# A transformer layer on one core: the two products with the same weights joined into one wide product, the first loads put in a new order

## The chip, the core and the metric

The kernel runs on one core of one Trainium2 chip. The core has TensorE (matrix products, written to PSUM), VectorE, ScalarE and GpSimd (element-wise work), and SyncE, whose queue here does nothing but issue loads and stores. The metric is the device time of one execution in microseconds (us), the median of three runs. A separate profiled execution gives the rows that are quoted below; times in them count from the start of its span.

## The reference

One layer, 256 rows of width 2048, all in float32. Three sublayers, each followed by a layer norm of (1.19 x input + result):

```python
h = x @ w_in                               # 2048 -> 7216 columns
(q_a, k_a, v_a, q_b, k_c, v_c, k_s, v_s, k_w, v_w, g_nsa, g_merge) = split(h)
y_a = swa_sink_attention(q_a, k_a, v_a)    # 16 heads, window 128, sinks, relative bias
y_b = nsa_attention(q_b, ...)              # 16 heads: compressed, selected and window keys, gated
merged = sigmoid(g_a) * (y_a @ w_branch_swa) + sigmoid(g_b) * (y_b @ w_branch_nsa)
x1 = layer_norm(ALPHA * x + merged @ w_mix_out)
x2 = layer_norm(ALPHA * x1 + cross_attention(x1, mem))   # 4 heads of 128
out = layer_norm(ALPHA * x2 + square(relu(x2 @ mlp_w1)) @ mlp_w2)   # 2048 -> 8192 -> 2048
```

The compressed keys and values are a small network of their own: 15 overlapping blocks of 32 tokens, 2048 -> 256 -> 64 with gelu between.

## The kernel before

**Split products.** Every large product is made from two parts of each operand: `h` is the value rounded to the format of the fast product, `l` the rest. A product of x and w is then h x xh + h x xl + l x xh. Weights come from memory in chunks of 128 x 1024 values (128 x 1072 for the keys and values). For each chunk ScalarE makes `h` (L168) and VectorE `l` (L169). Activations are split the same way when they are transposed (`hilo`, L322 and L323); `xth` and `xtl` hold the two parts of the transposed x, 16 blocks (k) of 128 x 256.

**Two forms.** `block_x` (`mm_x`, L201 to L208) keeps the activations as the fixed operand and streams up to 512 columns of weights. `block_w` (`mm_w`, L216 to L219) keeps a 128 x 128 tile of weights fixed and streams the 256 rows of x, so its result comes out transposed; it makes three products of 256 columns for each tile and each k, all into the same half of a PSUM bank. It is used for the two query blocks (`evac_qa`, `evac_qb`), the memory's keys and queries (512 columns each) and the first MLP stage (8 blocks of 1024 columns). The key/value chunks (`make_c`, 16 of them, one k each) do both: six products of 432 columns and fifteen of 256.

**Order.** The order of each engine's queue is written by hand. `run_chunks` goes through the list of chunks: it issues loads (five raw buffers), makes the splits up to three chunks ahead, emits the products of this chunk, then, at the end of a block, its evacuation. Chunks marked in `evac_first` leave one split for after the evacuation. Everything else (transposes, softmax, the compression chain) is a generator in `Side`: a `yield "pe"` gives the step that follows its place behind the products of a chunk, a `yield "ev"` before the next chunk's splits, `"ev0"` ahead of the other `"ev"` steps. A yield is thus a slot of the chunk loop, about 2.9 us long.

**The front.** x's first 256 columns, then chunk 0, x's next 256 columns, chunk 1 and so on are issued from SyncE, five loads a chunk; the other 1536 columns of x and a dozen small tables are issued from GpSimd. TensorE transposes x in pairs of blocks between the chunks (`x_side`). `small_start` makes the bias table after four slots.

**The compression chain** (`compress`) runs after the last of eight chunks that are set between those of the first query block: results `hid` copied, transposed on TensorE (`hidt`), gelu on VectorE and ScalarE (L554 to L564), then twelve small products into `kvc` (L570, L573). In the same slots the queries of the first attention are evacuated (`evac_q`, L310 and L315) and stacked (`stack_q`: ScalarE copies at L596, subtractions at L597, every other one on GpSimd).

**Banks.** PSUM has eight banks: four under the tag `acc`, and `lg`, `pt`, `o`, `mi`, which the side work uses. Before the MLP and within it, blocks alternate between the two sets; the blocks before use `acc` only, so that a block can begin a bank only when the block before has been copied out of it.

## Time and profile before

| | |
|---|---|
| median of three runs | 1442.91 us (1441.77 to 1443.74) |
| the profiled execution | 1444.05 us, of it 1442.3 us span |
| TensorE busy | 1412.6 us, 98% |
| VectorE, ScalarE, GpSimd busy | 875.2, 712.0, 174.5 us |
| moved by DMA | 268.58 MB, 186 GB/s over the span |
| mean granted TensorE clock | 0.99 of full |

The records of TensorE's products overlap, since a product starts while the one before drains; what a product costs in a row of them is the distance between two starts, not the length of a record. The granted clock is given as a share of 2.4 GHz.

### The profile page before, as it was taken

What the parts mean: (1) busy time and instruction counts of PE and PEld (TensorE: products, weight loads), DVE (VectorE), ACT (ScalarE), POOL (GpSimd) and SP (SyncE); (2) the same over time, 40 slices, a digit from 0 to 9 for tenths busy, and PEclk for the clock granted to TensorE, in tenths of its full rate; (3) what the DMA queues carried; (4) which work ended last, traced back from release to release, by engine and by line L of the source; (5) the groups of instructions that cost most, each with busy time, mean ns of one, the idle gap of its engine ahead of it and who ended that gap; (6) DMA issues with size and microseconds to landing.
All of it is one profiled execution on the core that took longest, in us unless ns stands there. A gap on an engine that the chain in (4) does not pass through costs nothing.

```text
span 1442.3 us, 22448 instructions
## 1 busy us (share of the span) xinstructions
PE 1412.6 (98%) x8732; PEld 1275.6 (88%) x8732; DVE 875.2 (61%) x1323; ACT 712.0 (49%) x1098; POOL 174.5 (12%) x165
## 2 busy tenths in 40 slices
PE   7999999999999999999999999999999999999996
PEld 6999988888888888899899999999998888888885
DVE  3577887888546466675854444444446555665556
ACT  3465776677444444454444444344445544544452
POOL 3002221221001010130201111011101000000002
PEclk9999999999999999999999999999999999999998
DMA  8765555454766575574355555665657666566552
GB/s 232 228 209 186 161 150 172 146 149 132 248 192 186 190 292 184 164 239 144 132 180 186 180 184 178 190 182 184 183 183 250 193 197 191 176 212 195 192 193 84
DMA packets 96282, 268.58 MB, mean 186 GB/s; under 512 B 9344, under 2 KB 32592, under 8 KB 95408
## 3 DMA queue, kind: packets, MB, share of 16 engines
q1 hardware_dynamic: 93344, 254.71, 56.5%
q0 software_dynamic: 2832, 12.45, 2.5%
q8 instruction: 68, 1.11, 0.3%
q14 instruction: 38, 0.31, 0.1%
HBM read 264.97 MB, written 2.15 MB: 185 GB/s over the span
## 4 chain that ended last, share of the span: by engine, by line
PE 66%; issue 25%; DVE 5%; ACT 2%; POOL 1%; DMA 1%; SPq 0%; ACTq 0%; DVEq 0%; POOLq 0%
PE acc L208 22%; PE acc L216 11%; PE acc L218 11%; PE acc L219 11%; DVE l L169 2%; PE acc L201 1%; PE acc L203 1%; PE acc L202 1%; DMA raw<-in_w_in_dram 1%; PE pt L662 1%; DVE p L635 1%; PE tr L337 0%; PE hid L528 0%; PE ntr L955 0%; PE o L671 0%
## 5 line engine op out<-in xcount | busy, mean ns | idle before, releaser
L169 DVE TENSOR_TENSOR l<-raw,h 128x1024 fp32r<-128x1024 f32 (+2 forms) x469 | 590.5, 1263 | 474.5 <-ACT h L168 466.3
L168 ACT CAST h<-raw 128x1024 fp32r<-128x1024 f32 (+2 forms) x469 | 490.2, 1048 | 534.6 <-PE acc L208 255.8
L216 PE MATMUL acc<-h2th,h 128*128 128x256 f32 x1024 | 291.3, 284 | 0.0
L218 PE MATMUL acc<-h2tl,h 128*128 128x256 f32 x1024 | 290.7, 284 | 0.0
L219 PE MATMUL acc<-h2th,l 128*128 128x256 f32 x1024 | 290.6, 284 | 0.0
L216 PEld LDWEIGHTS acc<-h2th,h 128*128 128x128 f32 x1024 | 197.6, 193 | 0.0
L218 PEld LDWEIGHTS acc<-h2tl,h 128*128 128x128 f32 x1024 | 197.5, 193 | 0.0
L219 PEld LDWEIGHTS acc<-h2th,l 128*128 128x128 f32 x1024 | 197.5, 193 | 0.0
L208 PE MATMUL acc<-l,ah 128*128 128x512 f32 x476 | 146.6, 389 | 0.0
L208 PE MATMUL acc<-h,ah 128*128 128x512 f32 x476 | 146.5, 389 | 0.0
L208 PE MATMUL acc<-h,al 128*128 128x512 f32 x476 | 146.5, 389 | 0.0
L208 PEld LDWEIGHTS acc<-l,ah 128*128 128x128 f32 x476 | 89.3, 188 | 18.6
L208 PEld LDWEIGHTS acc<-h,al 128*128 128x128 f32 x476 | 89.3, 188 | 18.6
L208 PEld LDWEIGHTS acc<-h,ah 128*128 128x128 f32 x476 | 89.3, 188 | 18.5
L216 PE MATMUL acc<-xth,h 128*128 128x256 f32 x336 | 97.5, 290 | 0.1
L219 PE MATMUL acc<-xth,l 128*128 128x256 f32 x336 | 96.7, 288 | 0.0
L218 PE MATMUL acc<-xtl,h 128*128 128x256 f32 x336 | 96.7, 288 | 0.0
L208 PE MATMUL acc<-h,xth 128*128 128x512 f32 (+1 forms) x252 | 81.2, 394 | 3.5 <-ACT h L168 3.5
L1148 POOL TENSOR_TENSOR a<-relu 128x512 f32<-128x512 f32 x32 | 44.3, 1412 | 314.6 <-ACT relu L1146 314.6
L208 PE MATMUL acc<-l,xth 128*128 128x512 f32 (+1 forms) x252 | 79.7, 388 | 0.6 <-DVE l L169 0.6
L208 PE MATMUL acc<-h,xtl 128*128 128x512 f32 (+1 forms) x252 | 79.5, 387 | 0.0
L216 PEld LDWEIGHTS acc<-xth,h 128*128 128x128 f32 x336 | 66.5, 198 | 0.6 <-ACT gt L483 0.2
(304 smaller groups left out, 2139.8 us busy)
## 6 DMA issues: line engine op xcount, KB each, us to landing
raw<-in_mlp_w_dram SPq DMA_DIRECT2D x256, 512.0 KB, 4.1
raw<-in_w_in_dram SPq DMA_DIRECT2D x96, 512.0 KB, 3.6
raw<-in_w_mix_out_dram SPq DMA_DIRECT2D x32, 512.0 KB, 4.2
raw<-in_w_branch_swa_dram SPq DMA_DIRECT2D x16, 512.0 KB, 3.6
raw<-in_w_branch_nsa_dram SPq DMA_DIRECT2D x16, 512.0 KB, 3.6
raw<-in_xa_w_kv_dram SPq DMA_DIRECT2D x16, 512.0 KB, 4.4
raw<-in_w_in_dram SPq DMA_DIRECT2D x48, 128.0 KB, 2.8
tbias<-udram POOLq DMA_DIRECT2D x8, 512.0 KB, 4.9
```

The costliest lines, as they stand in the source:

```text
L168: nc.scalar.copy(h[:, c0:c1], raws[c][:, c0:c1])
L169: nc.vector.tensor_sub(l[:, c0:c1], raws[c][:, c0:c1], fp(h[:, c0:c1]))
L201: nc.tensor.matmul(a, lhsT=xh(s), rhs=h[:, c0:c1], start=first, stop=False)
L202: nc.tensor.matmul(a, lhsT=xh(s), rhs=l[:, c0:c1], start=False, stop=False)
L203: nc.tensor.matmul(a, lhsT=xl(s), rhs=h[:, c0:c1], start=False, stop=last)
L208: nc.tensor.matmul(acc[s, b], lhsT=lhs(s), rhs=rhs[:, c0:c1], start=False, stop=False)
L216: nc.tensor.matmul(a, lhsT=h[:, c], rhs=xh, start=first and (t % 2 == 0 if opens is None else t in opens), stop=False)
L218: nc.tensor.matmul(a, lhsT=h[:, c], rhs=xl, start=False, stop=False)
L219: nc.tensor.matmul(a, lhsT=l[:, c], rhs=xh, start=False, stop=last and (t % 2 == 1 if closes is None else t in closes))
L635: nc.vector.tensor_tensor_reduce(p[:, c:c + w], lg[:, c:c + w], tbias[n.u][:, h, :w][:, ::-1], 1.0, -3e38, OP.add, OP.max, mx[:, i:i + 1])
L662: nc.tensor.transpose(pt[:, i * P:(i + 1) * P], p[:, b * P:(b + 1) * P], ident)
L1148: nc.gpsimd.tensor_mul(box["a"][k // KD][:, k % KD:k % KD + 2, :], two(r), two(r))
```

## The change

- `block_b` is new. The two parts of a block of activations now lie side by side in one tile (`Parts`, tiles of 8 k each), so that one product of 512 columns makes h x xh and h x xl, in the two halves of a bank; l x xh is added to the first half. The evacuation (`halves`) copies one half on ScalarE and adds the other on VectorE. `block_b` has four tiles of 128 columns, one bank each, and chunks of two k. It takes the place of `block_w` in the query blocks (two blocks of 512 each), the memory's keys and queries, and the first MLP stage but for its first 1024 columns. The square of relu moves from ScalarE and GpSimd to VectorE there (`evac_b`).
- The first loads: x's first piece is issued from ScalarE's queue, each key/value chunk by three loads instead of five (the columns are put in order by the split, `kv_parts`), the other pieces of x and the small tables from SyncE's queue between the chunks.
- Fillers of TensorE (`keep_warm`) are 512 columns wide; there are now nine around x's first transposes, and eight instead of twenty before the MLP.
- `compress` yields more slots before the gelu's end and before `kvc`; `small_start` waits for eight slots instead of four; x's later transposes come every second slot.
- `stack_q` subtracts on VectorE alone.
- Memory slots of the query stacks, `yt`, and the activations are dealt anew; `relu` and `al` have one buffer less.

```diff
-                nc.tensor.matmul(ps[:, :P], lhsT=idle, rhs=idle, start=True, stop=True)
+                nc.tensor.matmul(ps.rearrange("p (a n) -> p a n", a=4), lhsT=idle,
+                                 rhs=idle.unsqueeze(1).to_broadcast([P, 4, P]), start=True, stop=True)
...
-            for c0, c1 in ((512, ch.n), (0, 512)) if c == 0 else ((0, ch.n),):
-                nc.scalar.copy(h[:, c0:c1], raws[c][:, c0:c1])
-                nc.vector.tensor_sub(l[:, c0:c1], raws[c][:, c0:c1], fp(h[:, c0:c1]))
+            for src, dst in ch.parts:
+                nc.scalar.copy(dst(h), src(raws[c]))
+                nc.vector.tensor_sub(dst(l), src(raws[c]), fp(dst(h)))
...
+    def block_b(w, n0, rhs, evac, tags=("acc",) * 4, pre=None):
+        box = {}
+        for k0 in range(0, KD, 2):
+            def mm(h, l, k0=k0):
+                if k0 == 0:
+                    box["t"] = [bank(tag, "acc") for tag in tags]
+                for a in range(2):
+                    k = k0 + a
+                    for t, o in enumerate(box["t"]):
+                        c = slice((4 * a + t) * P, (4 * a + t + 1) * P)
+                        nc.tensor.matmul(o, lhsT=h[:, c], rhs=rhs.both(k), start=k == 0, stop=False)
+                        nc.tensor.matmul(o[:, :S], lhsT=l[:, c], rhs=rhs(k)[0], start=False, stop=k == KD - 1)
...
+    def halves(dst, t, scale=None):
+        if scale is None:
+            nc.scalar.copy(dst, t[:, S:])
+            nc.vector.tensor_add(dst, t[:, :S], dst)
...
-    load_x(0, 256)
+    nc.scalar.dma_start(out=xraw[:, :, :S], in_=x[:, :S].rearrange("(s p) n -> p s n", p=P))
...
-    for c in range(512, D, 512):
-        load_x(c, c + 512, nc.gpsimd)
...
-        for _ in range(4):
+        for _ in range(8):
             yield "pe"
...
-        return [(lambda r: halves(r[:, :1024])[:, :, :P], halves(rows[:, COL_KA:COL_KA + 256])),
-                (lambda r: r[:, 128:384], rows[:, COL_KC:COL_KC + 256]),
-                (lambda r: halves(r[:, 384:896])[:, :, :P], halves(rows[:, COL_KS:COL_KS + 256])),
-                (lambda r: r[:, 944:1072], rows[:, COL_KS + 256:COL_KS + 384]),
-                (lambda r: r[:, 768:944], rows[:, COL_KS + 384:COL_KS + 560])]
+        own = [(lambda r: r[:, 128:944], rows[:, COL_KC:COL_KC + 816]),
+               (lambda r: r[:, 0:128], rows[:, COL_KA:COL_KA + 128]),
+               (lambda r: r[:, 944:1072], rows[:, COL_VA:COL_VA + 128])]
+        pieces = {1: (1,), 2: (2,), 3: (3,), 4: (4,), 6: (5,), 8: (6,), 10: (7,)}.get(k, ())
+        more = [x_piece(m) for m in pieces] + small.get(k, [])
+        more = [(lambda r, t=t: t, src) for t, src in more]
+        return more + own if k == 1 else own + more
...
+        if k == 0:
+            return [pairs(1, 2), cols(896, 1072), pairs(0, 1), cols(0, 128)]
+        return [pairs(0, 2), cols(896, 1072), cols(0, 128)]
...
         nc.vector.tensor_mul(hq, hq, hx)
-        yield "ev"
+        yield "pe"
+        yield "ev0"
         nc.scalar.activation(hq, hq, AF.Tanh, scale=GELU_C)
...
-        yield "pe"
+        for _ in range(3):
+            yield "pe"
         yield from side.take("mi")
         ps = bank("mi", "kvc")
...
-            copy_any(raw[:, 2 * b:2 * b + 2, :], two(t))
-        return raw
+            halves(qraw[i][:, 4 * j + b, :], t)
+        return qraw[i]
...
-                (nc.gpsimd if e else nc.vector).tensor_sub(l_ap, src, fp(h_ap))
+                nc.vector.tensor_sub(l_ap, src, fp(h_ap))
...
-    block_w(w_in, COL_QA, 1024, xk, evac_qa)
+    block_b(w_in, COL_QA, xk, lambda tiles: evac_q(0, 0, tiles))
+    evac_first.add(len(chunks) - 1)
+    block_b(w_in, COL_QA + 512, xk, evac_qa)
...
-    block_w(w_in, COL_QB, 1024, xk, evac_qb, pre=lambda: side.require("stacks"))
+    block_b(w_in, COL_QB, xk, lambda tiles: evac_q(1, 0, tiles), pre=lambda: side.require("stacks"))
+    evac_first.add(len(chunks) - 1)
+    block_b(w_in, COL_QB + 512, xk, evac_qb)
...
-    block_w(xa_w_kv[0], 0, 512, mek, evac_t("kt", None))
+    block_b(xa_w_kv[0], 0, me, evac_t("kt", None))
+    evac_first.add(len(chunks) - 1)
...
-    block_w(xa_w_q[0], 0, 512, hk, evac_t("qt", 128 ** -0.5), pre=lambda: side.require("ln1"))
+    block_b(xa_w_q[0], 0, hk, evac_t("qt", 128 ** -0.5), pre=lambda: side.require("ln1"))
...
-        keep_warm(20, "mi")
+        keep_warm(8, "mi")
...
+    def evac_b(f):
+        def evac(tiles):
+            for b, t in enumerate(tiles):
+                r = box["pc"].tile([P, S], F32, tag="sum", name="sum", bufs=3)
+                halves(r, t)
+                k = 4 * f + b
+                nc.vector.scalar_tensor_tensor(box["a"][k // KD][:, k % KD, :], r, 0.0, r, op0=OP.max, op1=OP.mult)
+        return evac
...
-    for f in range(8):
-        block_w(mlp_w1[0], 1024 * f, 1024, hk, evac_a(f), tags=alt if f % 2 else ("acc",) * 4)
+    block_w(mlp_w1[0], 0, 1024, hk, evac_a(0))
+    for f in range(2, 16):
+        block_b(mlp_w1[0], 512 * f, hk, evac_b(f), tags=("acc",) * 4 if f % 2 else alt)
...
-    emit_load()
-    load_x(256, 512)
-    emit_load()
-    for c in range(512, D, 512):
-        emit_load()
+    emit_loads()
...
+    keep_warm(5, "mi")
-    for g in transpose_pairs(xraw, xth, xtl, range(1), "pt"):
+    for g in transpose_pairs(xraw, xk, range(1), "pt"):
         pass
+    keep_warm(4, "mi")
```

## Rows read from the trace of the kernel before

**Rows 1.** Page, part 1: busy time, share of the span and number of instructions of each engine.

```profile
PE 1412.6 (98%) x8732; PEld 1275.6 (88%) x8732; DVE 875.2 (61%) x1323; ACT 712.0 (49%) x1098; POOL 174.5 (12%) x165
```

**Rows 2.** The groups of TensorE's instructions by line, operands and shape; count, then busy time and mean ns of one record, then idle time before them.

```profile
L216 PE MATMUL acc<-h2th,h 128*128 128x256 f32 x1024 | 291.3, 284 | 0.0
```

**Rows 3.** Timeline of TensorE in the first MLP stage: start in us, length in us of the record, line, operation, operands, shape. The first and the last of 28 narrow products in a row.

```profile
799.75 0.28 PE L216 MATMUL acc<-h2th,h 128*128 128x256 f32 x1
...
802.99 0.28 PE L216 MATMUL acc<-h2th,h 128*128 128x256 f32 x1
```

**Rows 4.** The chain of work that ended last, in order of time, two of its longer pieces between 200 and 420 us: start in us, us, what, how many.

```profile
221.55 0.80 PE lgc L711 x8
...
374.00 38.08 PE acc L208 x168
```

**Rows 5.** Timeline of TensorE at the seam of the two shapes in a key/value chunk.

```profile
48.51 0.36 PE L208 MATMUL acc<-l,xth 128*128 128x432 f32 x1
48.70 0.36 PE L208 MATMUL acc<-h,xtl 128*128 128x432 f32 x1
48.90 0.28 PE L216 MATMUL acc<-xth,h 128*128 128x256 f32 x1
```

**Rows 6.** Waits of TensorE over the whole span: who waited for whom, us in total, times, longest.

```profile
PE tr L337 <- DMA xraw<-in_x_dram: 3.8, 1, 3.8
PE acc L208 <- ACT h L168: 3.5, 1, 3.5
PE kvc L570 <- DVE early L561: 1.7, 1, 1.7
PE kvc L573 <- DVE early L564: 0.9, 1, 0.9
```

**Rows 7.** Stretches in which the granted clock is at its lower level: length, busy time (and instructions) of TensorE, its weight loads, VectorE, ScalarE and GpSimd, then granted clock, DMA share and GB/s.

```profile
16.20:23.00 6.80, 5.25 (x18) 4.66 (x19) 3.06 (x3) 2.49 (x3) 0.31 (x1) 0.50 0.91 232
132.30:139.10 6.80, 6.60 (x31) 6.61 (x32) 5.37 (x14) 2.60 (x8) 0.00 (x0) 0.50 0.29 89
705.70:712.50 6.80, 6.01 (x27) 5.40 (x28) 5.63 (x11) 4.43 (x7) 3.60 (x4) 0.50 0.00 0
```

**Rows 8.** Timeline of TensorE at the front, matmuls alone: chunk 0's first product, three of its later ones, the second transposes of x, the first product of chunk 1 and that of chunk 2.

```profile
7.34 0.73 PE L201 MATMUL acc<-h,xth 128*128 128x432 f32 x1 [2.50 <-ACT h L168]
...
9.72 0.56 PE L203 MATMUL acc<-h,xtl 128*128 128x432 f32 x1
10.08 0.41 PE L216 MATMUL acc<-xth,h 128*128 128x256 f32 x1
10.30 0.41 PE L218 MATMUL acc<-xtl,h 128*128 128x256 f32 x1
...
13.07 0.60 PE L1215 MATMUL xtr<-ident,xraw 128*128 128x128 f32 x4
17.17 0.73 PE L208 MATMUL acc<-h,xth 128*128 128x432 f32 x1 [3.50 <-ACT h L168]
...
23.74 0.44 PE L208 MATMUL acc<-h,xth 128*128 128x432 f32 x1
```

**Rows 9.** DMA in the first 20 us: all packets, and the issues of chunk pieces of 128 KB (KB each, median us from issue to landing).

```profile
DMA packets 5741, 4.94 MB, mean 247 GB/s; under 512 B 625, under 2 KB 5277, under 8 KB 5741
...
raw<-in_w_in_dram SPq DMA_DIRECT2D x16, 128.0 KB, 3.0
```

**Rows 10.** Waits of SyncE's queue in the first 20 us.

```profile
SPq L151 <- DMA raw<-in_w_in_dram: 4.1, 3, 1.6
```

**Rows 11.** Timeline of TensorE around the compression chain's end: the last narrow product before it, and the first logits of the attention after it.

```profile
128.97 0.28 PE L219 MATMUL acc<-xth,l 128*128 128x256 f32 x1
...
134.22 0.56 PE L627 MATMUL lg<-kah,qs_a 128*128 128x256 f32 x1
```

**Rows 12.** Timeline of TensorE before the MLP: the fillers, and the transposes behind them.

```profile
702.22 2.34 PE L123 MATMUL warm<-idle 128*128 128x128 f32 x20
...
706.37 1.99 PE L955 MATMUL ntr<-ident,res 128*128 128x128 f32 x6 [1.56 <-DVE res L948]
```

**Rows 13.** Timeline of VectorE and GpSimd beside the compression chain.

```profile
124.14 0.29 DVE L556 TENSOR_TENSOR early<-early 128x128 f32<-128x128 f32 x1
...
124.83 3.04 POOL L597 TENSOR_TENSOR qs_a<-qraw,qs_a 64x512 fp32r<-64x512 f32 x2 [87.83 <-ACT qs_a L596]
...
128.46 1.23 DVE L169 TENSOR_TENSOR l<-raw,h 128x1024 fp32r<-128x1024 f32 x1
...
129.60 1.29 DVE L561 SCALAR_TENSOR_TENSOR early<-early 128x64 f32<-128x64 f32 x1
```

**Rows 14.** The same columns for three other stretches: the unpacking of the keys and values, the first layer norm, the first MLP stage.

```profile
72.00:92.00 20.00, 20.00 (x169) 20.00 (x169) 18.11 (x34) 13.05 (x21) 0.00 (x0) 1.00 0.54 161
600.00:626.00 26.00, 24.77 (x204) 23.99 (x204) 24.36 (x31) 17.67 (x24) 14.73 (x9) 1.00 0.48 145
710.00:1075.00 365.00, 365.00 (x3037) 365.00 (x3036) 168.91 (x140) 154.46 (x167) 47.34 (x34) 1.00 0.60 182
```

**Rows 15.** Groups by line and shape, as in rows 2: a ScalarE copy and a VectorE subtraction of 128x256 out of PSUM, and VectorE's own subtractions for the first query stack.

```profile
L541 ACT COPY early<-hid 128x256 f32<-128x256 f32 x1 | 0.4, 373 | 0.0
L323 DVE TENSOR_TENSOR h2tl<-ntr,h2th 128x256 fp32r<-128x256 f32 x4 | 1.7, 420 | 0.4 <-ACT h2th L322 0.4
L597 DVE TENSOR_TENSOR qs_a<-qraw,qs_a 64x512 fp32r<-64x512 f32 x4 | 4.7, 1204 | 0.1
```

More of the change, by code (lines that the diff above doesn't have):

```diff
@@ L43, with __init__ @@
 class Chunk:
-    def __init__(self, loads, n, mm, pre=None, with_split=None, post=None, cap=AHEAD, extra=None):
+    def __init__(self, loads, n, mm, pre=None, with_split=None, post=None, cap=AHEAD, extra=None, parts=None):
         self.loads, self.n, self.mm = loads, n, mm
@@ L47, in __init__, with part, __call__, both @@
         self.extra = extra
+        self.parts = parts or [((lambda r: r[:, :n]),) * 2]
+class Parts:
+    def __init__(self, *tiles):
+        self.tiles = list(tiles)
+    def part(self, i, k0, k1):
+        return self.tiles[k0 // 8][:, k0 % 8:(k1 - 1) % 8 + 1, i, :]
+    def __call__(self, k):
+        t = self.tiles[k // 8][:, k % 8]
+        return t[:, 0, :], t[:, 1, :]
+    def both(self, k):
+        return self.tiles[k // 8][:, k % 8].rearrange("p i s -> p (i s)")
 class Side:
@@ L515, in post @@
                 evac_c({"x0": a[0][:, :432], "x1": a[1][:, :432], "w0": a[2], "w1": a[3]})
-            chunks.append(Chunk(kv_loads(k), 1072, mm, post=post if k == KD - 1 else None))
+            chunks.append(Chunk(kv_loads(k), 1072, mm, post=post if k == KD - 1 else None, parts=kv_parts(k)))
     def make_cmp():
@@ L1024, in evac @@
             for b, t in enumerate(tiles):
-                copy_any(box[name][:, 2 * b:2 * b + 2, :], two(t), scale)
+                halves(box[name][:, b, :], t, scale)
             if name == "qt":
```

128 lines of the change are left out of this document (70 added, 58 removed).

## The prediction

> **What bounds the kernel now.** I read the page first: TensorE is busy for 98% of the span, VectorE for 61%, ScalarE for 49% [rows 1]. A busy TensorE is not yet a bound, since its records overlap, so I then read the distance between starts in the timeline. In the first MLP stage 27 narrow products (256 columns) start within 3.24 us, 0.120 us each [rows 3]; in the long stretches of wide products (512 columns) 168 of them take 38.08 us, 0.227 us each [rows 4]. The differences of the two fit a price per column plus some 13 ns per product: (0.227 - 0.120) / 256 is 0.417 ns a column, so 256 columns are 0.107 us and 13 ns are left. The products of 432 columns lie on the same line, 0.19 us apart by [rows 5] (180 + 13 ns), and where they alternate with narrow ones each keeps its own distance. So TensorE issues without a hole in both MLP stages, and what is left to gain there is the number of products alone.
>
> Then the list of waits of TensorE and the granted clock. The waits that last are few: at the front x's load and ScalarE's split, behind which stands a load, and at the compression's last product two waits on VectorE [rows 6]. After both, and once more before the MLP, the granted clock is at the lower level (0.50, 1.2 GHz) for 6.8 us [rows 7], and narrow products at that level start 0.21 us apart [rows 8].
>
> **1. Wide products.** Each narrow pair h x xh, h x xl becomes one wide product; l x xh stays narrow. Three products of 0.120 us (0.360) become 0.227 + 0.120 = 0.347 us: 13.3 ns less for each (k, tile). How many: 1024 in the first MLP stage [rows 2] less the 8 x 16 of its first block, which stays; by the loops of the code 2 x 8 x 16 in the query blocks, 4 x 16 for the memory's keys and as many for its queries. That is 1280, x 13.3 ns = 17.0 us. The columns streamed are the same; only 1280 issues go. Low end: in the 26 us around the first layer norm (most of the 64 pairs of the memory's keys) VectorE is busy for 24.4 of 26 us [rows 14], and what TensorE gains there may only be waited for: -0.9 us, so 16 to 17.
>
> The Trainium skill's page "TensorE: Matmul & The Clock Gate", section "Back-to-back issue gap", gives a distance of N/2.4 + 2.5 ns at the full clock: 109 and 216 ns. By it the pair saves 2.5 ns and the whole part 3.2 us instead of 17.0. The starts in [rows 3, 4] differ from it by 11 ns in both shapes, so the rows decide; it comes back as a rival.
>
> **2. The front.** Before: chunk 0's first product starts at 7.34 us and its narrow ones run at the low clock; then TensorE stands from 13.1 + 0.6 to 17.17 us for chunk 1's load, again for its low half, and runs chunk 1 at the low clock too; chunk 2 starts at 23.74 [rows 6 to 8]. The load is late because five small loads a chunk, the x pieces and POOL's large ones go at once (16 issues of 128 KB in rows of 512 B, mean 247 GB/s) and because SP waits for landings before it issues more [rows 9, 10]. After: three loads a chunk, one of 816 columns, x in pieces of 256 columns between them, POOL's loads gone from the front. Up to chunk 1 that is 2 x 549 KB and 2 x 262 KB, 1.62 MB; even at the old 247 GB/s 6.6 us, from about 2.7 us on (estimate: TensorE waits 3.8 us for x's first piece [rows 6], of which I take 1.1 for its transfer), so landed by 9.3 and split by 11. Chunk 0's first product: x's piece shares the engines with chunk 0 now but its parts are split in smaller steps; I take 7.0. Its 6 products of 432 and 15 of 256 take 2.9 us at the full clock, 5.4 at the low one (0.36 and 0.213 us each, [rows 8]). The fillers before it (five and four of 512 columns) keep TensorE at work while it waits for x and for chunk 0, so the clock may rise earlier. All low: 7.0 + 5.4 + 0.6 (transposes) + 2.9 + 0.4 gives chunk 2 at 16.3, a gain of 7.4. All full: 13.6, a gain of 10.1. I take the middle, 8.7, since TensorE has far more work ahead of chunk 0 than before but starts from rest. If chunk 1 lands only at 13, the gain is 5.
>
> **3. The compression chain and the stacks.** The last narrow product starts at 128.97; the first logits at 134.22 [rows 11]: 5.25 us that hold one narrow product and 12 tiny ones (0.1 us each by the eight of 0.80 us in [rows 4]), so 3.9 us are waiting (the list names 2.6 of it [rows 6], the low end). What it waits for stands in VectorE's rows: the chain's instruction on 128x64 takes 1.29 us while GpSimd subtracts for the query stack; one on 128x128 took 0.29 just before [rows 13]. Then the narrow products among the 31 of the low stretch [rows 7], some 22, run at 0.213 instead of 0.120: 2.0 us more. After: kvc comes two chunks later (the wait for the chain's tail lies under some 5.5 us of products), and nothing of GpSimd's runs beside it. VectorE takes over four subtractions of 64x512 for each stack, about 0.65 us each (half of the 1.23 us of 128x1024 in [rows 13]) where its own took 1.2 beside GpSimd's [rows 15]: 8 x 0.65 = 5.2 us against 4 x 1.2 = 4.8, hardly more than now. Gain 5.9. Splits run three chunks ahead (8 us) and cover that backlog; without it a late split costs what the backlog exceeds. Bounds: 6 at best, 4.6 by the list; 0 if the first logits wait for the stack instead and the clock falls again.
>
> The Trainium skill's page "SBUF — State Buffer", section "Who interferes with whom", says that a VectorE instruction with two SBUF inputs and a GpSimd one that reads SBUF exclude each other for a whole instruction. Rows 13 agree (1.29 for 0.29 us); by the rule the two of 1.3 us become 0.3 each, and 2 of the 3.9 us would go even without the extra slots; the rows give the same.
>
> **4. Fillers before the MLP.** 20 products of 128 columns (2.34 us) become 8 of 512 (1.8 us). The clock is low from 705.7 on, after fillers of 128 and an idle 1.56 us [rows 7, 12]; about 21 narrow products of the 27 there pay 0.093 us each, 2.0 us, and the transposes some 0.6. If the clock stays up, the next chunks soon wait for the transposed rows (VectorE's splits lie in between), so not all comes back: 0 to 2.6, I take 1.0.
>
> **5. What is added.** (a) Evacuation by halves: for each bank a ScalarE copy of 128x256 (0.37 us) and a VectorE sum (0.42, by the subtractions of 128x256 out of PSUM, [rows 15]) instead of one copy on either. In the MLP another VectorE product of that shape (0.42) in place of GpSimd's: 56 x 0.84 = 47 us more on VectorE, which is busy for 169 of 365 us [rows 14]: hidden, as the banks alternate. (b) Where they do not (key/value block to queries, three turns within and between the query blocks, queries to gates, the memory's keys and queries, MLP one to two: 8 turns) the four banks now close within 1.04 us instead of 2.2, and the new block wants bank after bank 0.35 us apart while VectorE frees one every 0.42. Bank 0 closes 1.04 us before the end and needs 0.28 + 0.37 + 0.42 = 1.07; the last one comes 0.25 late. With a split (1.23) queued ahead, 1.4. I take 0.4 each, 3.0 us; bounds 0 and 11. (c) Evacuating the key/value block in two parts: four more short instructions on each of two engines, in (b). Nothing in memory slots or the order of the MLP's loads (2 KB rows instead of 4 KB; 182 GB/s are asked [rows 14]) reaches the path.
>
> **Sum.** -17.0 - 8.7 - 5.9 - 1.0 + 3.0 = -29.6 us. The profiled execution took 1444.05 us (span 1442.3); 1414.5. It lies 1.1 above the median of the three runs, so the forecast is **1413 us**.
>
> **Rivals.** *The front is bound by supply*: SP still waits for landings, chunk 1 is split at 13 and x's later pieces lengthen chunks 2 to 4: gain 3 to 5, time 1417 to 1419. For it: SP's waits for landings [rows 10]; against: fewer and larger loads. *The chain's wait moves*: the first logits or a late split wait in its place and the clock drops again: 5.9 lost, 1419. For it: VectorE is busy for 18 of 20 us where the key/value results are unpacked [rows 14]. *More comes back*: the clock is up from the start and before the MLP, the turns cost nothing: -17.0 - 10.1 - 6 - 2.6, 1407. *A wide product buys nothing*: the 13 ns do not belong to the product, so the pair still takes 0.360: 1430. Against it: three widths on one line. (By the page's distance, part 1 above, it would be 1427.) *Slower*: the turns of (b). If at each of the 8 three splits (3.7 us) stand in VectorE's queue ahead of the sums and the clock falls behind each wait (2 us, as in part 3), they cost 46 instead of 3: 1456. It decides from 4.1 us a turn on. Against it: the turns of before show no wait in the list.
>
> **Numbers.** Forecast 0.46, supply 0.15, moved wait 0.14, more back 0.16, nothing from wide products 0.05, slower 0.04. A difference under 0.2% (2.9 us) cannot be told from none. Faster 0.94, same 0.02, slower 0.04. The range takes forecast, supply, moved wait (both at once: 1424) and more back: 1404 to 1423.
>
> **What would show it.** Starts in the MLP in pairs of 0.227 and 0.120 (else part 1 falls); chunk 2 at about 15 us and no load ended a wait of TensorE after chunk 0 (part 2); kvc without a wait and no low clock at 130 to 140 (part 3); the clock at about 680 us, before the MLP (part 4); gaps under 0.5 us at the 8 turns (5b). It is wrong above all if the turns cost microseconds or the low clock returns.

## The result, and the profile after

The changed kernel takes **1429.09 us** (median of four runs, 1428.18 to 1429.28) against 1442.72 for the kernel before beside it: ratio 0.9904, 95% interval 0.9887 to 0.9921. It is faster by 13.6 us. The forecast was 1413.0 with a range of 1404 to 1423, so the sign was right and the size was not: 16 us are missing, and the time lies outside the range. The profiled execution took 1429.11 us (span 1427.3) where the sum gave 1414.5 for it: 14.6 us.

Where they are missing is read from a few landmarks, the starts of the same products in both traces (us from the start of the span):

| from ... to | before | after | difference |
|---|---|---|---|
| start ... last product of 432 columns of the key/value block | 66.34 | 57.66 | -8.7 |
| ... last product into `hid` (compression) | 53.23 | 53.84 | +0.6 |
| ... first product into `lgc` (compressed logits) | 101.82 | 102.50 | +0.7 |
| ... first product of the first MLP stage | 486.62 | 485.50 | -1.1 |
| ... its last product | 373.14 | 365.82 | -7.3 |
| ... last product of all | 348.08 | 348.82 | +0.7 |

In this execution the front gave all that was forecast. The first MLP stage gave 7.3 where 896 pairs at 13.3 ns should have given 11.9, and the stage with the compression chain, from which 5.9 us were to come, became longer. (`hid` and `lgc` are the compression's first result and the logits of the compressed attention.)

TensorE's busy share is what it was [rows 1], so the page does not tell; its rows here are the engines' busy times:

```profile
PE 1400.3 (98%) x7449; PEld 1200.3 (84%) x7449; DVE 916.1 (64%) x1495; ACT 723.7 (51%) x1178; POOL 116.8 (8%) x115
```

The timeline of TensorE in the first MLP stage answers to [rows 3]: the wide product (L307) and the narrow one (L308), as start and length of record.

```profile
799.73 0.40 PE L307 MATMUL acc<-h2t,h 128*128 128x512 f32 x1
799.96 0.28 PE L308 MATMUL acc<-h2t,l 128*128 128x256 f32 x1
800.08 0.40 PE L307 MATMUL acc<-h2t,h 128*128 128x512 f32 x1
800.32 0.28 PE L308 MATMUL acc<-h2t,l 128*128 128x256 f32 x1
800.44 0.40 PE L307 MATMUL acc<-h2t,h 128*128 128x512 f32 x1
...
804.32 0.40 PE L307 MATMUL acc<-h2t,h 128*128 128x512 f32 x1
```

Thirteen pairs in 4.59 us are 0.353 us each, not 0.347, although nothing waits. The pairs are not equal either: by the nanosecond starts 349, 350, 361 and again (the expectation below that names 353 for the first of the three misread it). A pattern of three pairs takes 1060 ns where three times 346.7 would be 1040. All 14 blocks of wide products in this stage are like that; they are called blocks 2 to 15 below, since the stage's first 1024 columns, in narrow products, count as blocks 0 and 1.

TensorE's waits over the whole span answer to [rows 6], the stretch at the low clock to [rows 7]:

```profile
PE lg L695 <- DVE st L703: 2.2, 1, 2.2
...
PE tr L387 <- DMA xraw<-in_x_dram: 1.8, 1, 1.8
...
PE acc L307 <- ACT gt L538: 1.4, 2, 0.9
PE o L739 <- DVE ptl L373: 1.4, 5, 0.3
...
PE acc L220 <- DVE qraw L321: 0.8, 1, 0.8
```

```profile
127.60:131.00 3.40, 3.40 (x13) 2.80 (x12) 3.20 (x11) 2.65 (x9) 0.00 (x0) 0.51 0.81 258
```

The two waits of `kvc` are gone, and a wait of the attention's logits for VectorE stands in their place, with a new stretch at 1.2 GHz behind it. The low stretches of [rows 7] at the front and before the MLP are gone; the timeline at the front answers to [rows 8]:

```profile
7.95 0.47 PE L566 MATMUL acc<-h,xt 128*128 128x432 f32 x1
...
11.36 0.45 PE L227 MATMUL acc<-h,xt 128*128 128x432 f32 x1
...
14.79 0.44 PE L227 MATMUL acc<-h,xt 128*128 128x432 f32 x1
```

These are the first products of chunks 0, 1 and 2: chunk 2 begins at 14.79 (forecast 15.0), and no load ends a wait in between. In the 13 other profiles with the same front, of the runs below, it begins at 14.96 to 16.30.

### The profile page after: what moved, and what is told of

The parts are those of the page before. It is cut to its first block, busy times and chain, and to the rows that moved or that the text cites. A ratio compares the mean times of both kernels' runs of the same rounds, so it can differ in the third digit from the quotient of the medians.

```text
span 1427.3 us, 19977 instructions
## 1 busy us (share of the span) xinstructions
PE 1400.3 (98%) x7449; PEld 1200.3 (84%) x7449; DVE 916.1 (64%) x1495; ACT 723.7 (51%) x1178; POOL 116.8 (8%) x115
## 4 chain that ended last, share of the span: by engine, by line
PE 64%; issue 26%; DVE 6%; ACT 2%; POOL 1%; DMA 0%; POOLq 0%; ACTq 0%; DVEq 0%
PE acc L227 23%; PE acc L307 19%; PE acc L308 9%; DVE l L188 2%; PE acc L235 2%; PE acc L237 1%; PE acc L238 1%; PE acc L220 1%; PE acc L222 1%; PE acc L221 1%; PE pt L730 1%; POOL res L1012 1%; PE tr L387 1%; DVE res L1011 1%; PE hid L591 1%
## 5 line engine op out<-in xcount | busy, mean ns | idle before, releaser
L188 DVE TENSOR_TENSOR l<-raw,h 128x1024 fp32r<-128x1024 f32 (+4 forms) x501 | 585.1, 1177 | 410.3 <-ACT h L187 404.2
L187 ACT CAST h<-raw 128x1024 fp32r<-128x1024 f32 (+4 forms) x501 | 493.4, 994 | 490.8 <-PE acc L227 253.5
L307 PE MATMUL acc<-h2t,h 128*128 128x512 f32 x896 | 316.6, 399 | 0.0
L308 PE MATMUL acc<-h2t,l 128*128 128x256 f32 x896 | 251.6, 281 | 0.0
L307 PEld LDWEIGHTS acc<-h2t,h 128*128 128x128 f32 x896 | 168.4, 188 | 42.1
L308 PEld LDWEIGHTS acc<-h2t,l 128*128 128x128 f32 x896 | 169.3, 189 | 0.0
L227 PE MATMUL acc<-h,xt 128*128 128x512 f32 (+1 forms) x504 | 143.5, 389 | 0.0
L227 PEld LDWEIGHTS acc<-h,xt 128*128 128x128 f32 x504 | 93.1, 188 | 16.3
L307 PE MATMUL acc<-xt,h 128*128 128x512 f32 x256 | 93.3, 404 | 1.4 <-ACT gt L538 1.4
L227 PE MATMUL acc<-l,xt 128*128 128x512 f32 (+1 forms) x252 | 79.2, 386 | 0.0
L308 PE MATMUL acc<-xt,l 128*128 128x256 f32 x256 | 72.5, 283 | 0.0
L307 PEld LDWEIGHTS acc<-xt,h 128*128 128x128 f32 x256 | 48.9, 191 | 12.8 <-ACT gt L538 1.9
```

The costliest lines, as they stand in the source:

```text
L187: nc.scalar.copy(dst(h), src(raws[c]))
L188: nc.vector.tensor_sub(dst(l), src(raws[c]), fp(dst(h)))
L227: nc.tensor.matmul(acc[s, b], lhsT=lhs(s), rhs=rhs[:, c0:c1], start=False, stop=False)
L307: nc.tensor.matmul(o, lhsT=h[:, c], rhs=rhs.both(k), start=k == 0, stop=False)
L308: nc.tensor.matmul(o[:, :S], lhsT=l[:, c], rhs=rhs(k)[0], start=False, stop=k == KD - 1)
```

## Experiments on the pair

The first four runs ask what the 6.6 ns too many belong to: the change of width, the bank that two neighbours share, the wide product itself, or its operands.

**Widths grouped.** For each k the four wide products in a row, then the four narrow ones.

```diff
-                    for t, o in enumerate(box["t"]):
-                        ...wide product of tile t, narrow product of tile t
+                    for o, c in zip(box["t"], cs):
+                        nc.tensor.matmul(o, lhsT=h[:, c], rhs=rhs.both(k), ...)
+                    for o, c in zip(box["t"], cs):
+                        nc.tensor.matmul(o[:, :S], lhsT=l[:, c], rhs=rhs(k)[0], ...)
```

> The changed kernel, but for each k block_b makes its four wide products first and then the four narrow ones, instead of wide and narrow by turns. In the changed kernel a pair takes 0.355 us (0.237 from a wide start to the narrow one, 0.118 on), 8 ns more than the 0.347 of my sum. Theory A (the turn of shapes, or the loading of the wide product's weights under the short narrow one, costs the 8 ns): wide products 0.227 apart, narrow ones 0.120, a pair 0.347 to 0.350 on average, 1280 x 6 to 8 ns = 8 to 10 us faster than the changed kernel, 1419 to 1421. Theory B (a wide product that streams activations costs 0.237 in any order): unchanged pair of 0.355, 1429. Theory C (the narrow product follows in the bank that the wide one has just written): as A here, told from A by the next run.

Measured: 1430.27 us (1428.84 to 1430.73), ratio 0.9904 [0.9889, 0.9919]. A pair takes 350.8 ns in every block. 2.5 of the 6.6 ns went, not all, so the change of width is not the whole cause. The MLP stage became 1.8 us shorter (364.0 instead of 365.82); the kernel as a whole did not, since its profile is 1.5 us later at the front and 1.1 later between `lgc` and the MLP.

**Narrow product one tile later.** The narrow product of tile t is issued behind the wide one of tile t + 1, so that, but for the last of a chunk, two neighbours write different banks.

> The changed kernel, but each narrow product of block_b comes one place later, after the wide product of the next tile, so that it never follows the wide product of its own bank (but for the last of a chunk); wide and narrow still come by turns. Theory C (same bank): a pair back at 0.347, 9 us faster than the changed kernel, 1420. Theories A and B: still 0.355, 1429.

Measured: 1428.67 us (1428.44 to 1429.05), ratio 0.9895 [0.9879, 0.9912]; 352.5 ns a pair. The bank is not the cause.

**Wide product undone.** The same block in the same order, with two narrow products in place of the wide one: three products for each k and tile.

> The changed kernel, but each wide product of block_b is two narrow ones into the two halves of the bank again; all else of the change stays. By the distances measured in the changed kernel (0.355 for a pair against 0.360 for three narrow ones) it is 1280 x 5 ns = 6 us slower than the changed kernel, 1435; by the 13 ns of my sum it would be 17 us slower, 1446. If wide products bring nothing at all: 1429.

Measured: 1438.21 us (1437.98 to 1439.09), ratio 0.9962 [0.9947, 0.9977]: three products in 360.0 ns, as before the change. All wide products together are worth 9.1 us, where 17.0 were forecast, and 1280 x 6.6 ns is 8.4.

**Seven kinds of pair in one kernel**, two MLP blocks each: weights as the wide product's moving rows, activations as its fixed operand, zeros as its moving rows, one tile of weights for both, two activation blocks that do not lie side by side, both products wide. The kernel then no longer computes the layer.

> A measurement of distances alone; results of the MLP are not the layer's. The changed kernel, but the wide product of block_b takes other operands in the MLP's blocks, two blocks each, in this order: as it is; streaming weights (the first 512 columns of the split chunk) instead of activations; activations as the fixed operand, streaming activations; streaming zeros; both products with the same fixed weights; streaming two blocks of xh that don't lie side by side; both products wide. Before it the wide product that streams the pair of activations stands 0.234 to 0.237 from the next start, the wide ones that stream weights (block_x) 0.227. Theory B1 (what is streamed sets it): 0.227 with streamed weights and with zeros, 0.234 or more with fixed activations and with the same weights. Theory B2 (the fixed operand sets it: weights that are loaded while a long stream runs): 0.227 with fixed activations, 0.234 or more with streamed weights and zeros. Theory B3 (the values set it: random values against zeros): 0.227 with zeros only. Theory A again (shapes by turns): 0.227 when both are wide.

Measured in one execution (ns per pair, and wide to narrow + narrow to wide):

| as it is | weights moving | activations fixed | zeros moving | same weights | not side by side | both wide |
|---|---|---|---|---|---|---|
| 236.3 + 117.0 = 353.4 | 236.3 + 117.0 = 353.3 | 236.1 + 117.3 = 353.4 | 226.1 + 120.7 = 346.8 | 231.7 + 115.0 = 346.7 | 231.5 + 115.2 = 346.7 | 453.4 |

None of the single causes fits: zeros are fast, but so are both kinds behind them, which have nothing in common with zeros. What the three fast kinds share is the order in which they came. That suggested another reading, and the traces bear it out: in the first query block, from about 63 to 84 us, the same code ran at 353.3 in the kernel after and at 346.7 in others. Here is that stretch in the kernel after, the wide products at both ends of 59 pairs:

```profile
63.00 0.40 PE L307 MATMUL acc<-xt,h 128*128 128x512 f32 x1
...
83.85 0.40 PE L307 MATMUL acc<-xt,h 128*128 128x512 f32 x1
```

And here in the kernel with the spread stack (below), the first pair of 59 in a row and the wide products behind it and at the end:

```profile
63.94 0.39 PE L307 MATMUL acc<-xt,h 128*128 128x512 f32 x1
64.17 0.28 PE L308 MATMUL acc<-xt,l 128*128 128x256 f32 x1
64.28 0.39 PE L307 MATMUL acc<-xt,h 128*128 128x512 f32 x1
...
84.39 0.39 PE L307 MATMUL acc<-xt,h 128*128 128x512 f32 x1
```

20.85 us for 59 pairs are 0.3534 us each; 20.45 us are 0.3466, every pair alike. So one and the same stream has two steady rhythms, called gaits here. Nor is it the small edit that sets the gait in this place: four profiles have the code of the kernel after up to the MLP, and two of them run this stretch at 353 (the kernel after, and the run with products of zeros ahead of blocks 4 to 14), two at 346.7 (the run with seven kinds, and the kernel after with one start). The block begins behind two waits, of 0.5 and 0.9 us.

**What sets the gait in the MLP: products of zeros ahead of blocks.** One to twenty products of zeros are added ahead of blocks 4 to 14.

> Timing probe with the layer's results kept: extra products of a tile of zeros are put ahead of blocks 4 to 14 of the first MLP product, the kernel after otherwise. In the traces so far the same pair of instructions runs at 346.7 ns in some stretches (wide to narrow 230, narrow to wide 117: 59 pairs on end in the stretch 63.9 to 84.4 us of the run with the spread stack) and at 353.3 in others (a pattern that repeats every three pairs: 353, 350, 361), all MLP pairs of the kernel after among them, which begin right behind a run of products of 256 columns. Theory P (what runs ahead of a block decides which of the two patterns it falls into, and it keeps it until something else breaks the stream): behind four wide zero products (block 4, 10, 12) and behind pairs of zeros (block 8) the 64 pairs run at 346.7; behind twelve products that end in eight narrow ones (blocks 5, 7, 9, 11, 13) they run at 353.3 again. Theory Q (the pair of full operands always falls back to 353; only the operands of zeros, or what the blocks of the earlier probe did instead, ran faster): all blocks 353 to 354 whatever is ahead. Theory R (one step into the fast pattern lasts): from the first block that is at 346.7 on, all later ones are, resets too.

Measured in one execution: blocks 4, 5, 7, 10 and 12 to 15 at 346.7 ns, blocks 2, 3, 6, 8, 9 and 11 at 353.3, each from its first pairs to its last. The gait is chosen at the block's entry and then kept: block 3 keeps that of block 2 and block 15 that of block 14, which have nothing between them. The rule that I gave for the choice (wide zeros make it fast, narrow ones slow) fails: blocks 5, 7 and 13 are fast behind a run that ends in narrow products, and blocks 6 and 8 slow.

**Zeros ahead of block 2 alone**, on the kernel with the joined edits (below).

> The kernel of the joined edits with four wide products of zeros more, one into each bank ahead of the first wide block (block 2) of the first MLP product; the results are unchanged. In the last probe four such products ahead of a block brought its pairs from 353.3 to 346.8 ns, and a block with nothing ahead kept the pattern of the one before it. Theory P (what runs ahead of a block decides the pattern, and the pattern stays): if block 2 falls into the fast one, all 14 blocks run at 346.8, 14 x 64 x 6.5 ns = 5.8 us less, for 0.9 us of zeros: 1421.7 (1420.5 to 1423). By the probe's thirteen blocks with products ahead or without, 7 of 11 with products ahead were fast, so P leaves a chance of about 4 in 10 that block 2 stays slow here, and then every block is slow and the time is 1427.5; what P rules out is a mixture. Rival Q (the fast pattern decays by itself in the longer run, or evacuations push it out at the turns): some blocks fast and later ones slow with nothing ahead, 1423 to 1427.

Measured: 1427.51 us (1426.11 to 1427.85). All 14 blocks stay at 353.3. There is no mixture, as the reading asks, but this run alone would also fit a gait that nothing moves; the four products that made block 4 fast did not do it for block 2.

**Another start in each block.** No product more or less; the first one to three steps over k of blocks 2 to 12 are issued in groups of two or four.

```diff
+                    g = steps.get(k, 1)
+                    for t in range(0, 4, g):
+                        ...g wide products in a row, then their g narrow ones
...
+            2: {0: 4}, 3: {0: 2}, 4: {0: 4, 1: 4}, 5: {0: 2, 1: 2}, 6: {0: 4, 1: 4, 2: 4}, 7: {0: 4, 1: 2},
+            8: {0: 2, 1: 4}, 9: {0: 4, 2: 4}, 10: {0: 4}, 11: {0: 2}, 12: {0: 4, 1: 4}}
```

> The kernel of the joined edits; no product more or less, but the first one to three products over k of blocks 2 to 12 of the first MLP product are issued in another order (two or four wide products in a row, then their narrow ones), a different one in each block; blocks 13 to 15 are as they were. Theory P: the step between a grouped start and the pairs behind it can change the pattern, so blocks differ, each either at 346.7 or at 353.3 throughout, and blocks 13 to 15 stay as block 12 leaves them; with half of the blocks fast 2.9 us less than the joined kernel: 1423.7 (1421 to 1426.6). Rival Z (it takes products of zeros, whose moving rows are one tile read four times, to get into the fast pattern): all blocks at 353.3, 1426.6.

Measured: 1424.04 us (1423.38 to 1425.87). Behind their starts blocks 2, 5, 7 and 9 run at 346.7 ns, the others at 353.2 to 353.4, and 13 to 15 as block 12 left them. So zeros are not needed. The same start gave 346.7 in block 2, which came behind narrow products, and 353.4 in block 10, which came behind fast pairs: it is the stream before and the start together that decide.

**One start, block 2 alone**, on the joined kernel and on the kernel after:

```diff
-        block_b(mlp_w1[0], 512 * f, hk, evac_b(f), tags=("acc",) * 4 if f % 2 else alt)
+        block_b(mlp_w1[0], 512 * f, hk, evac_b(f), tags=("acc",) * 4 if f % 2 else alt, steps={2: {0: 4}}.get(f, {}))
```

> The joined kernel with one edit: in the first step over k of the first wide block (block 2) of the first MLP product the four wide products are issued in a row and then their four narrow ones; all other pairs as they were, no product more or less. In the run with a different start in each block this start brought block 2 to 346.7 ns per pair. Theory P (a pattern stays until the order of the stream changes): all 14 blocks at 346.7, first MLP product 896 x 6.6 ns = 5.9 us shorter than in the joined kernel, 1420.7 (1419.7 to 1422). Rival D (the turns between blocks, with bank waits of their own, drop the stream back after some blocks): a mixture, 1421.5 to 1426.5. Rival L (the entry depends on chance, not on the code ahead): block 2 at 353.3 this time, and all behind it, 1426.6.

> The kernel after with that same single edit at block 2 of the first MLP product. Theory P, with an entry that the code sets: all 14 blocks at 346.7 as in its companion, 1429.1 less 5.9 = 1423.2 (1422 to 1424.5). Rival L (chance): 353.3 in one of the two kernels, and 1429.1 for it.

Measured: **1420.49 us** (1419.19 to 1421.11), ratio 0.9838 [0.9823, 0.9853], and on the kernel after 1422.76 us (1422.46 to 1422.99), ratio 0.9855 [0.9839, 0.9872]. The timeline of the first: the start of block 2, then the first products of blocks 3 and 15.

```profile
746.09 1.09 PE L309 MATMUL acc<-h2t,h 128*128 128x512 f32 x4
747.02 0.63 PE L311 MATMUL acc<-h2t,l 128*128 128x256 f32 x4
747.49 0.40 PE L309 MATMUL acc<-h2t,h 128*128 128x512 f32 x1
...
768.29 0.39 PE L309 MATMUL acc<-h2t,h 128*128 128x512 f32 x1
768.52 0.28 PE L311 MATMUL acc<-h2t,l 128*128 128x256 f32 x1
...
1034.53 0.39 PE L309 MATMUL acc<-h2t,h 128*128 128x512 f32 x1
1034.76 0.28 PE L311 MATMUL acc<-h2t,l 128*128 128x256 f32 x1
```

From 768.29 to 1034.53 there are 12 blocks of 64 pairs: 266.24 us / 768 = 346.7 ns. Four wide products in a row, once, are worth 6.3 us on the kernel after and 6.1 on the joined kernel (896 x 6.6 ns is 5.9). Block 2 was fast in all three profiles with this start and slow in all eight with the usual one. It begins without a wait, right behind narrow products 0.120 us apart, so the entry is set by the code there and not by chance, unlike that of the query block. Both kernels beat the two that were compared at first.

## Experiments on the stage of the compression chain

VectorE's timeline in the kernel after shows where the wait of 2.2 us comes from; it answers to [rows 13]. Four subtractions of the stack stand in two places (x4 is four instructions), the splits of the chunks (L188) behind them, and the row maxima (L703) last.

```profile
116.99 2.84 DVE L665 TENSOR_TENSOR qs_a<-qraw,qs_a 64x512 fp32r<-64x512 f32 x4
119.86 1.23 DVE L188 TENSOR_TENSOR l<-raw,h 128x1024 fp32r<-128x1024 f32 x1
121.01 0.22 DVE L625 SCALAR_TENSOR_TENSOR early<-early 128x64 f32<-128x64 f32 x1
...
121.72 2.84 DVE L665 TENSOR_TENSOR qs_a<-qraw,qs_a 64x512 fp32r<-64x512 f32 x4
124.59 1.23 DVE L188 TENSOR_TENSOR l<-raw,h 128x1024 fp32r<-128x1024 f32 x1
125.73 0.42 DVE L703 CUSTOM_DVE_ANT_0 p<-lg,tbias 128x256 f32<-128x256 f32 x1
```

On TensorE, in answer to [rows 11], the first logits now come at 120.87, ahead of `kvc`, and fill bank `lg`; the second ones must wait for the maxima that read it:

```profile
121.23 0.28 PE L696 MATMUL lg<-kal,qs_a 128*128 128x256 f32 x1
...
124.06 0.28 PE L308 MATMUL acc<-xt,l 128*128 128x256 f32 x1
126.56 0.39 PE L695 MATMUL lg<-kah,qs_a 128*128 128x256 f32 x1 [2.21 <-DVE st L703]
```

**The first stack spread**: four slots of two subtractions instead of two of four.

```diff
-                if (e == 0 and b % 2 == 0) or qs is qs_b:
+                if e == 0 or qs is qs_b:
```

> The changed kernel, but the first query stack is made in four slots of two subtractions each instead of two slots of four. Theory: the 2.4 us wait of the second logits (for the bank that VectorE's row maxima release) and the 3.4 us at the low clock behind it come from VectorE's queue being full with eight subtractions and two splits; with half as many a slot the wait and the low stretch vanish, 3 to 4 us faster than the changed kernel, 1425. Rival: VectorE is the bound of this stage anyway and the wait only moves to a later slot: 1428 to 1430, with a wait of TensorE on VectorE elsewhere between 115 and 145 us.

Measured: 1426.18 us (1425.06 to 1427.09), ratio 0.9877 [0.9863, 0.9892], 2.9 us below the kernel after. The wait is off the list, the clock stays at 2.4 GHz between 120 and 145 us, and `lgc` begins at 211.07 instead of 214.00. From `hid` to `lgc` it is 99.0 us instead of 102.5. The clock's part in this has to be taken off: in the three other profiles that have the code of the kernel after up to the MLP the logits wait 2.2 us just the same, the clock stays up, and the stage takes 101.0. So the wait is worth 2.0 us and the low stretch, which came behind the same wait in one of four profiles, 1.5. The edit also moves the first logits two slots on, to 128.35, behind all eight subtractions; leaving the stack as it was and moving the logits alone was not tried.

**GpSimd back on the stack**: every other subtraction there, as in the kernel before; all else as in the kernel after.

> The changed kernel, but every other subtraction of the query stacks is on GpSimd again. Theory: it is the three slots, not the engine, that took the compression chain's wait away; VectorE's instructions are stretched again beside GpSimd's (1.2 us instead of 0.7 for a subtraction), so its queue is as long as with eight of its own and the second logits wait all the same: 1428 to 1430. Rival: the second logits wait because VectorE makes all eight; with four the wait is gone, 1425 to 1426.

Measured: 1431.24 us (1431.08 to 1431.49), ratio 0.9913 [0.9897, 0.993], 2.2 us above the kernel after (the intervals overlap; the four runs of each do not). VectorE's and GpSimd's timelines there:

```profile
121.04 3.63 POOL L665 TENSOR_TENSOR qs_a<-qraw,qs_a 64x512 fp32r<-64x512 f32 x2 [0.58 <-DVE qs_a L665]
122.18 1.32 DVE L625 SCALAR_TENSOR_TENSOR early<-early 128x64 f32<-128x64 f32 x1
123.42 1.34 DVE L627 SCALAR_TENSOR_TENSOR early<-early 128x64 f32<-128x64 f32 x1
...
127.58 0.42 DVE L703 CUSTOM_DVE_ANT_0 p<-lg,tbias 128x256 f32<-128x256 f32 x1
```

The chain's instruction takes 1.32 us beside GpSimd's subtractions (121.04 to 124.67) and 0.22 without: the lengthening of [rows 13] is GpSimd's doing. The GpSimd subtractions that stood beside the chain's instruction in the kernel before are not the ones in [rows 13] but the next two:

```profile
128.50 3.54 POOL L597 TENSOR_TENSOR qs_a<-qraw,qs_a 64x512 fp32r<-64x512 f32 x2 [0.62 <-DVE qs_a L597]
```

The maxima come 1.85 us later, 0.6 of it because this execution was later at `hid`, and the logits wait 3.4 instead of 2.2. In the stage, from `hid` to `lgc`, this is 1.3 us more (103.8 against 102.5, both with a low stretch of 3.4).

**The chain's old slots**, with the stack on VectorE alone.

> The changed kernel with the compression chain's old slots. Theory: without GpSimd beside it the chain is short enough that the twelve small products wait only about 1 us for VectorE's copy (it ends 0.8 us after the slot in the changed kernel), and what follows waits that much less: 1429 to 1431. Rival: the chain stands behind four subtractions and a split in VectorE's queue and costs 4 us and more again with a low clock behind it: 1432 to 1435.

Measured: 1428.16 us (1427.77 to 1428.24), ratio 0.9891 [0.9876, 0.9906]: 0.9 below the kernel after, which the intervals do not tell from nothing. `kvc` waits 0.2 us there and the logits 1.1. So taking GpSimd off cured `kvc`'s wait; the three slots more were not needed.

**Three edits joined**: the spread stack, the chain's old slots, and at the turn from the key/value block to the queries the gates' tanh ahead of the value split, and the next chunk's split behind both.

> The kernel after with three edits of the earlier runs joined: the first query stack's subtractions spread over four slots (1426.2, 2.9 below after), the compression chain's old slots (0.9 below after), and the turn behind the compressed keys' and gates' product: the gates' tanh goes ahead of the value split in that evacuation, and the next chunk's split behind it, as at the other turns. Theory: the edits are in different places, so that their gains add: the two waits of the query product for the gates' tanh (0.7 and 1.05 us) fall to under 0.5 each, so first product of the query block 1.0 to 1.3 earlier; second logits wait under 0.3; median 1424.3 (1423.3 to 1425.5). Rival: the turn's waits stay, because the value split's own steps (ScalarE and VectorE in turn, 2.35 us for each half) are what holds the bank: 1425.3. Rival: the chain's old slots make the logits wait again, since its two gains have one cause: 1426.2 less the turn, 1425.2.

Measured: 1426.60 us (1426.16 to 1426.98), ratio 0.9885 [0.9868, 0.9901]. `lgc` begins at 210.77, 0.3 before that of the spread stack alone; the turn's wait fell from 1.4 to 0.9 us (now for VectorE's half of the value split), and no more. The median is that of the spread stack alone within the noise and above all three figures expected: the gains do not add. That two of the edits work on one wait, the second logits', fits this. It is the base of the two runs on the pair above.

## An experiment on the fillers

The fillers of the kernel before: none at the front, 20 of 128 columns before the MLP.

> The changed kernel with the fillers of the kernel before: none at the front, twenty of 128 columns before the MLP. Theory: at the front chunk 0 runs at the low clock (0.36 us instead of 0.19 for a product of 432 columns), 1.5 to 2.5 us later at chunk 2; before the MLP the low stretch is 6.8 us again, against none in the changed kernel's profile and 3.4 us in those of three of its variants, 1 to 2 us: 1431 to 1433. Rival: the order of the loads alone brings the front's 8.7 us and the clock falls and rises as it will: 1429.

Measured: 1431.58 us (1430.01 to 1432.35), ratio 0.9914 [0.9899, 0.9928], 2.5 us above the kernel after. Its waits:

```profile
PE tr L386 <- DMA xraw<-in_x_dram: 5.4, 1, 5.4
...
PE acc L565 <- ACT h L186: 1.3, 1, 1.3
```

The clock rises at 13.2 us there, at 8.17 in the kernel after and at 8.35 to 11.12 in the other profiles with the new fillers. The last product of 432 columns starts at 59.93 instead of 57.66 in the kernel after, and 57.83 to 59.17 in the others: at the front the fillers are worth 0.8 to 2.3 us, with one profile without them. The loads in their new order bring the rest by themselves: chunk 2 begins at 17.07 in this run, against 23.74 [rows 8]. Before the MLP the clock was low for 3.4 us with the old fillers; but so it was in 9 of the 14 profiles with the new ones, and not in that of the kernel after. What sets it there stays open.

## Why the prediction was wrong, step by step

**Part 1, the wide products: the mechanism right, the price per pair wrong.** 1280 x 13.3 ns = 17.0 us were forecast; undoing them is worth 9.1. The step that failed is the pair's 0.347 us as the sum of two distances, each of which had been read where only its own shape runs [rows 3, 4]. By turns the wide product took 236.3 ns and the narrow one 117.0, in place of 226.7 and 120.0. The sum does exist (346.7 ns, and 15.4 us for all the pairs when the MLP's run in it: 9.1 + 6.3), but the alternating stream can also lock into 353.3, and the kernel after enters the MLP's blocks in that gait. The evidence offered for the sum, wide and narrow products that keep their distances at a seam [rows 5], was one change of width, and by the nanosecond starts the distances were not steady there: 189 to 198 for the products of 432 columns, 113 to 121 for the narrow ones. It says nothing of a stream that changes width at each product. This is 7.9 of the 14.6 us.

**Part 3, the chain and the stacks: the rival came true.** 5.9 us were forecast, with "0 if the first logits wait for the stack instead and the clock falls again". It was the second logits. `kvc`'s waits (2.6 us in [rows 6]) and a low stretch of 6.8 us [rows 7] went; a wait of 2.2, a low stretch of 3.4 in which a pair takes 0.64 us, and softmax waits of 2.2 in place of 0.3 came. The stage lost 0.7 us instead of gaining, though 136 pairs lie in it, each of which was to save 13.3 ns; in the three profiles of the same code in which the clock stayed up it gained 0.8. So the wait came in every one of them, the fall of the clock in one of four. The step that failed counted VectorE's work (5.2 us against 4.8) but not where it stands: four subtractions in a row are 2.84 us in one slot, and what is behind them in the queue is the row maxima that free the logits' bank. The splits ran ahead as said; the maxima do not. With the same work spread, and all of it ahead of the first logits (1426.18), 2.9 us come back. From 5.9 less to 0.7 more is 6.6 us in the profile, so that the two steps together are nearly the whole miss there (5.1 where the clock stayed up).

**Part 2, the front: right in the main**, 8.7 of 8.7 in this profile. The clock rises at 8.17 us, within chunk 0, the earliest of 14 profiles with the same front. In these the last product of 432 columns starts at 57.7 to 59.2, 58.5 in the middle, a gain of 7.8; so about 1 us of the agreement is luck. Most of it is the loads, 0.8 to 2.3 us the fillers.

**Part 4**: forecast 1.0. The way from `wo`'s first product to the MLP's takes 29.46 us instead of 29.76, and no low stretch follows, which accounts for the 1.4 us that the MLP stage gave beyond its pairs (7.3 less 896 x 6.6 ns = 5.9). About 1.7, within the bounds; but the low stretch comes in 9 of 14 profiles with these fillers, so that it was absent here is luck, and no run shows that the fillers have a part in it.

**Part 5b, the turns**: 3.0 forecast for eight. The first, from the key/value block to the queries, costs 1.7 us by the distances of starts, 1.4 in the list (two late banks, for the gates' tanh), queries to gates 0.8, the MLP's two stages 0.3: about 3 in all, but unevenly, and the dearest one by the value split (c), which had no price of its own in the sum. No turn fell near the 4.1 us at which the slower rival would have decided.

The range failed because the two misses came together: it went up to 1423, about what supply and moved wait at once would have given, and held a pair that buys nothing for one case in twenty, with no case for a pair that buys half.

## What to carry to other kernels

Price a stream of alternating shapes from a row where they alternate; in these runs the sum of two steady distances was the least that a pair took, not what it took as a rule. When work is moved onto an engine that has room on the whole, ask what stands behind it in that queue in its slot, and deal it out in pieces no longer than what waits can bear. If a stream without a wait is slower than its parts, look at the single distances for a repeating pattern, and try another first step of the same products.

## What the hardware showed that was not expected

A stream of wide and narrow products, each with its own weights, has two lasting gaits: 346.7 ns a pair (all alike, or 350 and 343 by turns), or 353.3 in a pattern of three (349, 350, 361). In the MLP it stays in the one that it enters across block ends, evacuations and hundreds of microseconds (896 pairs), until the order of products changes; one step of four wide and four narrow products was enough to change it. Wide products alone keep 226.7 ns, narrow ones alone 120.0. Why there are two is not settled: it is not the bank and not the operands' values. The query block, which begins behind two waits, ran in either gait with the same code (two profiles each), so there it is not the code alone that chooses; what does, was not found.

The Trainium skill's page "TensorE: Matmul & The Clock Gate", section "Back-to-back issue gap", gives N/2.4 + 2.5 ns for an isolated product of N columns, which the prediction used, and about 131 ns for one of 512 columns in a stream with weight loads. In these runs 512 columns took 226.7 ns in a row of their own and 226 to 236 on average beside narrow ones, so neither figure fits, and the distance depends on what runs beside it. The Trainium skill's page "SBUF — State Buffer", section "Who interferes with whom", says that a VectorE instruction with two SBUF inputs contends with a GpSimd one that reads SBUF. The 1.32 and 0.22 us of one and the same instruction, with GpSimd's subtraction beside it and without, agree.
